# Result tiles worked on in steps, one per product, and later behind their transfer; weight splits three ahead

## The chip, the cores and the metric

The kernel runs on one core of a Trainium2 chip. The metric is the device time of one execution in microseconds.

## The reference

One layer of a hybrid encoder runs over two sequences, a prompt of 512 tokens and a sample of 1024, both 2048 wide, in float32 with shared weights. Cut to what is computed:

```python
h = rms_norm(x, norm_g)
z = h @ w_in                                   # 2048 x 5632
c_val, c_glu, c_gate, q, k, v, a_gate = split(z)   # 1024 x3, 1024, 256, 256, 1024
q, k = rope(q), rope(k)
u = c_val * sigmoid(c_glu)
u = depthwise_conv31(u) + b_dw                 # along the tokens
conv_out = (silu(layer_norm(u)) @ w_pw) * silu(c_gate)
attn_out = banded_sink_attention(q, k, v) * silu(a_gate)   # 8 heads, 2 kv heads, window 128
y = rms_norm(x + concat(conv_out, attn_out) @ w_out)
```

## The kernel before

Every float32 product is made of three passes over operands that are split into a high and a low part (`parts`, L352 on ACT for the high, L353 on DVE for the low part), so weights and activations have to be split before TensorE can use them.

**Units.** The input projection of the sample runs in 44 `Unit`s of 84 matmuls. A unit multiplies a 2 by 2 arrangement of blocks (two columns of weights, two halves of the tokens) by a Strassen-like scheme: seven products (`SUMS`, `OPERAND`) of 12 matmuls each, which accumulate in three PSUM banks (`BANK`: a for the products 0, 2, 4 and 6, b for 1, c for 3 and 5). Four prepared weight tiles feed the seven products: `make0` to `make3` form sums of raw weights on DVE (L136) and split them into one of three hl buffers (`NHL = 3`). After each product `tap` takes the bank's contents: after products 0, 2, 3 and 6 as a copy on ACT into a new result tile (L210), after 1, 4 and 5 as an addition on DVE (L212). Product 6 goes on in the bank that product 4 has filled, so it waits for the tap of product 4; product 5 waits in the same way for the copy of product 3's bank. The taps of a product are issued (`late`) after the first three matmuls of the next product.

**Four stages of units.** The units run in four stages: the convolution's 8 units over the first half of the depth, then over the second half, then the 14 other units (gates, keys, values, queries) over the second half and over the first. In the first and third stage a result tile is stored to DRAM (`part`). In the second and the fourth the unit has a `done`: the other half is added to the result tile in SBUF by an accumulating transfer from GpSimd's queue (`add_into`, L343), and the finished tile is then worked on and stored. In the stages 1, 2 and 4 the first two units are interleaved (`side`).

**The work on a result tile** depends on what it is. For the convolution (`gated`): scaled by the RMS factor R on DVE (L741), Sigmoid on ACT (L742), scaled again on DVE (L743) for the GLU column; multiplied with its partner of the value column (L747) and stored (`h_d`). For gates (`silu_of`): scaled (L756), Silu on ACT (L761), stored. For queries and keys (`rotate`): four DVE instructions of `rope` (L808 to L811), stored. For values (`value_of`): scaled (L756), then transposed by a lane.

**When it is issued.** `tap` puts `[LANDING, done]` on the list `later`. In each product, after the taps and the split of weights, `turn_over` counts all entries down by one and issues those at zero, whole: all of a tile's DVE and ACT instructions, at raised priority (`urgently`, `high_priority(URGENT)`). `turn_over` first calls `mark`, which notes the last instruction so far of DVE and of ACT; whatever is issued in `behind` (the work on result tiles, and the lanes with conv taps, attention and other background work) is put behind these on the same engine. Before the first job, `later` is emptied.

**Order.** A scheduler puts the instructions of each engine in order, by priority and by when buffers come free; the engines then run their queues in that order and wait on semaphores. The `Unit`s prepare weights one ahead: `product` asks for tile i at its start, and at every second product for `i + NHL - 1`, which means up to tile i + 1.

**The rest.** The prompt's projection and the three later parts (`Job`, L484, and `last_run`, L1230) run after the units. Conv taps (L780) are background work on DVE, paced by credit per product. Result tiles live in two pools of four buffers, g and u, that `E` hands out in turn.

Of the kernel before, what the change touches and what calls it, by code (L numbers as in the profile page):

```python
# [32 lines left out]
URGENT = 400  # L33
# [2 lines left out]
SOON = 800  # L36
PM = 30
RUSH = 1.45
LANDING = 3
LOAD = 4500  # L40
SPREAD = 3
RATES = (0.4, 0.6, 0.3, 1.0)
# [2 lines left out]
NT, NRAW, NHL = 28, 3, 3  # L45
# [40 lines left out]
class Unit:  # L86
# [82 lines left out]
    def product(self, step, late):  # L169
        e, nc = self.e, self.e.nc  # L170
        p, o = OPERAND[step]
        i = self.at[p]
        e.w_prep(i + 1)
        hl = e.hl[i]
        n = BANK[step]
        if step in FRESH:
            self.bank[n] = e.PS(self.tags[n], [W])
        acc = self.bank[n]
        toks = e.T[SUMS[step]]
        for j in range(HALF):  # L180
            for q, (l, r) in enumerate(((0, 0), (0, 1), (1, 0))):
                nc.tensor.matmul(  # L182
                    acc,
                    hl[:, l, o, j, :],
                    toks[j][:, r],
                    start=step in FRESH and j == 0 and q == 0,
                    stop=step in LAST and j == HALF - 1 and q == 2,
                    skip_group_check=True,
                )
            if j == 0:  # L190
                for fn in late:
                    fn()

                if step % 2 == self.side:
                    e.w_prep(i + NHL - 1)
                e.turn_over()
            e.tick(3 * MM)
        if step in (1, 3, 5, 6):
            e.hl.pop(i)
        for fn in self.after.get(step, ()):  # L200
            fn()
        return [lambda: e.urgently(self.tap, step)]

    def tap(self, step):
        e, nc = self.e, self.e.nc
        n = ((0, 0), (0, 0), (0, 1), (1, 1), (1, 1), (0, 1), (1, 0))[step]
        bank = self.bank[BANK[step]]
        if step in (0, 2, 3, 6):
            self.d[n] = e.E()
            nc.scalar.activation(self.d[n], bank, AF.Copy)  # L210
        else:
            nc.vector.tensor_tensor(self.d[n], bank, self.d[n], ALU.add)  # L212
        if step in (1, 4, 5, 6):
            part, d = self.part[n[0]][n[1]], self.d.pop(n)
            if self.done:

                e.add_into(d, part)
                e.later.append([LANDING, lambda: self.done(n[0], n[1], d)])
            else:
                e.store(part, d)  # L220

# [51 lines left out]
class Encoder:  # L273
# [108 lines left out]
    def turn_over(self, all=False):  # L382

        self.mark()
        for n, entry in enumerate(self.later):
            entry[0] -= 1
        while self.later and (all or self.later[0][0] <= 0):
            with self.behind():
                self.urgently(self.later.popleft()[1])


    def constants(self):
# [162 lines left out]
class Sequence:  # L555
# [177 lines left out]
    def gated(self, i):  # L733

        e, nc = self.e, self.e.nc
        held, made = {}, []

        def done(t, c, z):
            R = self.R[:, t * W : t * W + W]
            if c == 0:  # L740
                nc.vector.tensor_tensor(z, z, R, ALU.mult)  # L741
                nc.scalar.activation(z, z, AF.Sigmoid)  # L742
                nc.vector.tensor_tensor(z, z, R, ALU.mult)  # L743
            held[t, c] = z
            if (t, 1 - c) in held:
                g, v = held.pop((t, 0)), held.pop((t, 1))
                nc.vector.tensor_tensor(v, v, g, ALU.mult)  # L747
                e.store(self.h_d[i][:, t * W : t * W + W], v)
                made.append(t)
                if len(made) == 2:  # L750
                    e.conv.add(self.taps(i))

        return done
# [4 lines left out]
    def silu_of(self, dst):  # L758
        def done(t, z):
            self.scaled(z, t)  # L760
            self.e.nc.scalar.activation(z, z, AF.Silu)  # L761
            self.e.store(dst[:, t * W : t * W + W], z)

        return done
# [52 lines left out]
    def rotate(self, dst):  # L817
        def done(t, z):
            self.e.store(dst[:, t * W : t * W + W], self.rope(z, t, z))

        return done

# [6 lines left out]
    def value_of(self, g):  # L829
        def done(t, z):  # L830
            self.scaled(z, t)
            self.e.attn.add(self.turn_value(g, t, z))

        return done

# [639 lines left out]
```

## Time and profile before

| | us |
|---|---|
| median of 3 runs | 2267.61 (2260.0 to 2270.22) |
| the profiled execution's own time | 2265.19 |
| its span, first to last instruction | 2263.4 |
| PE busy in the span | 2158.1 |
| DVE busy in the span | 1650.3 |
| ACT busy in the span | 968.8 |
| mean granted TensorE clock | 0.982 |

The profile is of one execution. PE is the matrix engine, PEld its loads of weights, DVE the vector engine, ACT the scalar engine, POOL GpSimd, SP the queue that issues most transfers. A row of the groups gives line, engine, operation, written and read tiles with their shape and the count; then the busy time, the mean in ns of one, and the engine's idle time just ahead of these instructions with what ended it. A row of the waits reads "engine line waited for: us in total, times, longest". A row of the timeline gives the start, the length, engine, line and operation, and in brackets the idle time before it and its releaser. The stages of units end, in this execution, at 180.9, 370.7, 648.1 and 975.0 us.

### The profile page before, as it was taken

The numbers are of one execution on the slowest core, as the hardware profiler recorded it, in microseconds if no ns is written. First come the engines' busy times: TensorE is split into PE (matmuls) and PEld (weight loads), VectorE is DVE, ScalarE is ACT, GpSimd is POOL, SyncE is SP. The second block draws the span as 40 slices with busy tenths as digits, with TensorE's granted clock in tenths as the row PEclk, the third lists the DMA queues.
The fourth block names the chain that finished last, engine by engine and source line by source line (L and its number), as shares of the span: only waits on it lengthen the run. The fifth ranks groups of instructions, "written<-read, shape, count | busy, mean of one in ns | idle before, by whom it ended". The sixth has DMA issues, their size and how long they took to land.

```text
span 2263.4 us, 26350 instructions
## 1 busy us (share of the span) xinstructions
PE 2158.1 (95%) x9510; PEld 1764.4 (78%) x9510; DVE 1650.3 (73%) x2497; ACT 968.8 (43%) x1488; POOL 76.9 (3%) x92
## 2 busy tenths in 40 slices
PE   6999888999999898989999999999999999999998
PEld 5887677788877676778888888888888778888886
DVE  8657777898898788789998668868774586546343
ACT  5465334333353232453444555754463454423232
POOL 0001111000001111100000000000000000000000
PEclk8999999999999999999999999999999999999999
DMA  8967757664566555675444644347543366527342
GB/s 286 321 222 225 192 147 202 243 234 150 185 218 158 144 143 124 166 245 174 163 140 142 203 140 140 131 137 249 196 131 126 130 195 233 172 98 259 104 131 75
DMA packets 207748, 400.12 MB, mean 177 GB/s; under 512 B 18944, under 2 KB 76672, under 8 KB 207616
## 3 DMA queue, kind: packets, MB, share of 16 engines
q1 hardware_dynamic: 194944, 375.35, 49.8%
q0 software_dynamic: 12672, 23.07, 6.5%
q8 instruction: 74, 1.21, 0.2%
q14 instruction: 58, 0.48, 0.1%
HBM read 294.02 MB, written 104.33 MB: 176 GB/s over the span
## 4 chain that ended last, share of the span: by engine, by line
PE 58%; issue 14%; DVE 5%; DMA 4%; POOL 2%; ACT 1%; SPq 0%; POOLq 0%; ACTq 0%; DVEq 0%
PE a L484 20%; PE b L484 10%; PE c L484 10%; PE a L182 3%; PE pv L923 2%; PE a L1230 2%; PE s L1230 2%; DVE f L780 2%; PE s L891 2%; PE c L182 2%; DMA raw<-w_in 1%; PE pt L928 1%; DVE hl L353 1%; PE pv L1230 1%; PE b L1230 1%
## 5 line engine op out<-in xcount | busy, mean ns | idle before, releaser
L353 DVE TENSOR_TENSOR hl<-raw,hl 128x1024 fp32r<-128x1024 f32 (+1 forms) x323 | 371.6, 1150 | 219.6 <-ACT hl L352 210.8
L352 ACT ACTIVATE hl<-raw 128x1024 fp32r<-128x1024 f32 (+1 forms) x323 | 322.7, 999 | 487.3 <-PE a L484 95.0
L182 PE MATMUL a<-t,hl 128*128 128x512 f32 x1968 | 488.2, 401 | 44.3 <-DVE g L212 27.5
L484 PE MATMUL a<-t,hl 128*128 128x512 f32 x2112 | 510.4, 393 | 1.5 <-DVE hl L353 1.5
L182 PEld LDWEIGHTS a<-t,hl 128*128 128x128 f32 x1968 | 379.2, 194 | 134.8 <-DVE g L212 34.5
L780 DVE SCALAR_TENSOR_TENSOR f<-f,c_w_dw,f 128x1024 f32<-128x1024 f32 (+1 forms) x464 | 453.9, 1012 | 2.7 <-ACT f L776 1.6
L484 PEld LDWEIGHTS a<-t,hl 128*128 128x128 f32 x2112 | 393.0, 188 | 80.6 <-DVE hl L353 1.9
L182 PE MATMUL c<-t,hl 128*128 128x512 f32 x984 | 252.2, 405 | 29.7 <-ACT g L210 21.5
L484 PE MATMUL b<-t,hl 128*128 128x512 f32 x1056 | 253.6, 392 | 1.9 <-DVE a L1083 1.9
L484 PE MATMUL c<-t,hl 128*128 128x512 f32 x1056 | 251.9, 391 | 0.0
L182 PEld LDWEIGHTS c<-t,hl 128*128 128x128 f32 x984 | 192.1, 196 | 75.6 <-ACT g L210 24.0
L484 PEld LDWEIGHTS b<-t,hl 128*128 128x128 f32 x1056 | 196.7, 188 | 41.6 <-DVE a L1083 2.3
L484 PEld LDWEIGHTS c<-t,hl 128*128 128x128 f32 x1056 | 197.2, 188 | 40.1 <-DVE a L1083 0.3
L182 PE MATMUL b<-t,hl 128*128 128x512 f32 x492 | 119.4, 391 | 0.0
L182 PEld LDWEIGHTS b<-t,hl 128*128 128x128 f32 x492 | 92.8, 189 | 19.3
L136 DVE TENSOR_TENSOR raw<-raw,raw 128x512 f32<-128x512 f32 x123 | 84.5, 687 | 24.1 <-DMA raw<-w_in 16.2
L210 ACT ACTIVATE u<-a 128x512 f32<-128x512 f32 x76 | 45.2, 595 | 96.0 <-PE a L182 94.0
L905 ACT ACTIVATE p<-p,tiny 128x384 f32<-128x384 f32 (+1 forms) x96 | 54.6, 570 | 52.7 <-DVE tiny L902 52.6
L1230 PE MATMUL a<-hl,t 128*128 128x512 f32 x192 | 74.7, 390 | 0.0
L352 ACT ACTIVATE a<-pt 128x512 fp32r<-128x512 f32 x64 | 38.1, 596 | 79.6 <-PE pt L928 79.5
L353 DVE TENSOR_TENSOR a<-pt,a 128x512 fp32r<-128x512 f32 x64 | 44.0, 687 | 27.4 <-ACT a L352 26.8
L210 ACT ACTIVATE g<-a 128x512 f32<-128x512 f32 x47 | 27.9, 595 | 78.4 <-PE a L182 76.8
(244 smaller groups left out, 2189.5 us busy)
## 6 DMA issues: line engine op xcount, KB each, us to landing
raw<-w_in SPq DMA_DIRECT2D x169, 512.0 KB, 4.5
raw<-w_out SPq DMA_DIRECT2D x64, 512.0 KB, 3.8
raw<-w_out SPq DMA_DIRECT2D x64, 256.0 KB, 3.2
raw<-w_pw SPq DMA_DIRECT2D x24, 512.0 KB, 3.6
f<-xT_s SPq DMA_DIRECT2D x38, 256.0 KB, 5.8
f<-x_s SPq DMA_DIRECT2D x16, 512.0 KB, 6.2
f<-x_p SPq DMA_DIRECT2D x13, 512.0 KB, 6.4
u<-q_d SPq DMA_DIRECT2D x24, 256.0 KB, 4.3
```

Source lines behind the costliest of these rows:

```text
L136: self.e.nc.vector.tensor_tensor(out, x, y, ALU.subtract)
L182: nc.tensor.matmul(acc, hl[:, l, o, j, :], toks[j][:, r], start=step in FRESH and j == 0 and q == 0, stop=step in LAST and j == HALF - 1 a ...
L210: nc.scalar.activation(self.d[n], bank, AF.Copy)
L352: nc.scalar.activation(hi, x, AF.Copy)
L353: nc.vector.tensor_tensor(lo, x, hi.bitcast(F32), ALU.subtract)
L484: nc.tensor.matmul(job.acc[0], hl[:, l, kk // HALF, kk % HALF, :], r, start=i == 0 and p == 0, stop=i == nk - 1 and p == 2,)
L780: nc.vector.scalar_tensor_tensor(t, h[:, j : j + T], w(j), t, ALU.mult, ALU.add)
L891: nc.tensor.matmul(ps[:, 0:n], qs[:, x, h], k[y][:, keys], start=p == 0, stop=p == 2)
L905: nc.scalar.activation(p[:, 0:n], p[:, 0:n], AF.Exp, bias=nm[:, h : h + 1], accum_out=l[:, h : h + 1])
L923: nc.tensor.matmul(pv, v[x][:, vs], pt[:, y], start=i == 0 and p == 0, stop=i == last and p == 2)
L928: nc.tensor.transpose(tp[:, h], p[:, i * P : (i + 1) * P], e.ident)
L1230: nc.tensor.matmul(acc, self.mix[self.KS[i]][:, m, b * P : (b + 1) * P], part[l].rearrange("p a b -> p (a b)"), start=i == 0 and p == 0, s ...
```

## The change

Three things change.

- `done` becomes a generator. Each `turn_over` runs one step of every tile that is due, up to the next `yield`; the yields stand where the work goes from DVE to ACT or back, and at the end of the functions that have no such place. A tile is taken from the list when its generator ends. Tiles that are due no longer wait for the first in the list.
- `LANDING` goes from 3 to 4: the first step of a tile is issued one product later behind the transfer.
- `product` asks for `i + NHL`, up to weight tile i + 2, in every product and not in every second one for up to i + 1.

```diff
-LANDING = 3
+LANDING = 4
...
             if j == 0:
                 for fn in late:
                     fn()
-
-                if step % 2 == self.side:
-                    e.w_prep(i + NHL - 1)
+                e.w_prep(i + NHL)
                 e.turn_over()
...
                 e.add_into(d, part)
-                e.later.append([LANDING, lambda: self.done(n[0], n[1], d)])
+                e.later.append([LANDING, self.done(n[0], n[1], d)])
...
     def turn_over(self, all=False):
 
         self.mark()
-        for n, entry in enumerate(self.later):
+        for entry in list(self.later):
             entry[0] -= 1
-        while self.later and (all or self.later[0][0] <= 0):
-            with self.behind():
-                self.urgently(self.later.popleft()[1])
+            if all or entry[0] <= 0:
+                with self.behind():
+                    with self.tc.high_priority(URGENT):
+                        if next(entry[1], self) is self:
+                            self.later.remove(entry)
...
             if c == 0:
                 nc.vector.tensor_tensor(z, z, R, ALU.mult)
+                yield
                 nc.scalar.activation(z, z, AF.Sigmoid)
+                yield
                 nc.vector.tensor_tensor(z, z, R, ALU.mult)
...
     def silu_of(self, dst):
         def done(t, z):
             self.scaled(z, t)
+            yield
             self.e.nc.scalar.activation(z, z, AF.Silu)
             self.e.store(dst[:, t * W : t * W + W], z)
...
     def rotate(self, dst):
         def done(t, z):
             self.e.store(dst[:, t * W : t * W + W], self.rope(z, t, z))
+            yield
...
         def done(t, z):
             self.scaled(z, t)
             self.e.attn.add(self.turn_value(g, t, z))
+            yield
```

## The prediction

> **What bounds the kernel now.** I read the page first, then a table of the busy time by stage, then in the two stages that stand out the groups by line, the waits, and the timeline of one unit.
>
> ```profile
> span 2263.4 us, 26350 instructions
> PE 2158.1 (95%) x9510; PEld 1764.4 (78%) x9510; DVE 1650.3 (73%) x2497; ACT 968.8 (43%) x1488; POOL 76.9 (3%) x92
> ...
> 56.50:113.10 56.60, 56.60 (x252) 46.88 (x250) 37.54 (x50) 25.14 (x37) 0.00 (x0) 1.00 0.94 321
> ...
> 0.00:180.90 180.90, 163.06 (x677) 130.75 (x678) 125.81 (x197) 99.06 (x154) 0.20 (x4) 0.95 0.79 271
> 180.90:370.70 189.80, 164.89 (x674) 131.87 (x673) 138.67 (x177) 67.78 (x97) 26.70 (x31) 0.94 0.67 178
> 370.70:648.10 277.40, 271.31 (x1180) 221.72 (x1179) 237.97 (x291) 107.81 (x151) 1.28 (x2) 0.99 0.64 212
> 648.10:975.00 326.90, 288.47 (x1194) 232.16 (x1193) 264.85 (x344) 125.26 (x180) 47.86 (x55) 0.95 0.63 160
> 975.00:2263.40 1288.40, 1270.38 (x5793) 1047.86 (x5791) 882.97 (x1491) 568.85 (x907) 0.88 (x1) 1.00 0.49 160
> ```
>
> The windows give length, then busy time and count of PE, PEld, DVE, ACT and POOL, then the granted clock. The kernel is PE's: 95% busy. An undisturbed stretch runs 252 matmuls in 56.6 us, 0.2246 us each. At that price the second stage (674 matmuls) needs 151.4 us and takes 189.8; the fourth (1194) needs 268.2 and takes 326.9. These two, the ones with POOL work, are the only stages where units call `done`, and they lose 38.4 + 58.7 = 97.1 us. The first stage loses some 29 us, mostly its start; the third 277.4 - 265.0 = 12.4; the last, over half the span, loses nothing that this change reaches. DVE has the next claim: 264.85 us of work in the fourth stage against PE's 268.2.
>
> ```profile
> L741 DVE TENSOR_TENSOR g<-g,f 128x512 f32<-128x512 f32 x8 | 5.5, 692 | 10.3 <-DMA g<-part_conv 10.3
> L741 DVE TENSOR_TENSOR u<-u,f 128x512 f32<-128x512 f32 x7 | 4.8, 689 | 5.6 <-DMA u<-part_conv 5.6
> L747 DVE TENSOR_TENSOR u<-u,g 128x512 f32<-128x512 f32 x5 | 3.5, 692 | 14.2 <-DMA u<-part_conv 14.2
> L747 DVE TENSOR_TENSOR g<-g,g 128x512 f32<-128x512 f32 x2 | 1.4, 692 | 2.6 <-DMA g<-part_conv 2.6
> ...
> L756 DVE TENSOR_TENSOR u<-u,f 128x512 f32<-128x512 f32 x17 | 11.7, 690 | 16.9 <-DMA u<-part_q 10.8 <-DMA u<-part_kv 4.6 <-DMA u<-part_gate 1.5
> L756 DVE TENSOR_TENSOR g<-g,f 128x512 f32<-128x512 f32 x16 | 11.0, 691 | 16.3 <-DMA g<-part_q 9.2 <-DMA g<-part_gate 4.7 <-DMA g<-part_kv 2.4
> L808 DVE TENSOR_TENSOR g<-g,f 64x512 f32<-64x512 f32 x10 | 6.9, 687 | 6.9 <-DMA g<-part_q 5.1 <-DMA g<-part_kv 1.5
> L808 DVE TENSOR_TENSOR u<-u,f 64x512 f32<-64x512 f32 x9 | 6.2, 687 | 9.6 <-DMA u<-part_q 7.8 <-DMA u<-part_kv 1.7
> ```
>
> The last field is DVE's idle time ahead of the group: the first readers of a result tile stand waiting for the accumulating transfer, 32.7 us in the second stage (first four rows) and 49.7 in the fourth. DVE idles 189.8 - 138.67 = 51.1 us there in the second and 326.9 - 264.85 = 62.05 in the fourth, so these waits are most of it. Two timelines show how PE pays, first in the second stage, then in the fourth:
>
> ```profile
> 290.93 0.69 DVE L741 TENSOR_TENSOR g<-g,f 128x512 f32<-128x512 f32 x1 [2.05 <-DMA g<-part_conv]
> 291.66 0.63 ACT L742 ACTIVATE g<-g 128x512 f32<-128x512 f32 x1 [6.09 <-DVE g L741]
> 292.19 0.58 ACT L210 ACTIVATE g<-c 128x512 f32<-128x512 f32 x1
> 292.82 4.40 PE L182 MATMUL c<-t,hl 128*128 128x512 f32 x12 [3.18 <-ACT g L210]
> ...
> 822.44 0.88 POOL L343 DMA_DIRECT2D u<-part_q  x1 [9.47 <-DVE u L212]
> 826.25 0.69 DVE L808 TENSOR_TENSOR u<-u,f 64x512 f32<-64x512 f32 x1 [1.09 <-DMA u<-part_q]
> 829.61 1.22 DVE L353 TENSOR_TENSOR hl<-raw,hl 128x1024 fp32r<-128x1024 f32 x1
> 830.74 0.68 DVE L212 TENSOR_TENSOR g<-a,g 128x512 f32<-128x512 f32 x1
> 831.48 7.34 PE L182 MATMUL a<-t,hl 128*128 128x512 f32 x24 [4.09 <-DVE g L212]
> ```
>
> Above, ACT stands six microseconds at the Sigmoid (L742), which waits for DVE, which waits for the transfer; the copy of bank c (L210) is queued behind it, and PE waits for that bank. Below, the transfer issued at 822.44 holds DVE until 826.25, the rotation follows, and the add that frees bank a (L212) ends so late that PE stands 4.09 us. It is a loop: late tap, late transfer, late rotation, next late tap.
>
> ```profile
> PE c L182 <- ACT g L210: 17.8, 5, 6.3
> PE a L182 <- DVE g L212: 23.9, 10, 4.3
> PE s L182 <- ACT hl L352: 7.7, 3, 3.4
> 292.80:296.30 3.50, 3.48 (x9) 0.57 0.00 0
> DMA to landing us min/median/max: 3.8/4.6/8.8
> ```
>
> The first two rows are those stalls, in the second and in the fourth stage; the third, of the whole span, is all that a split's high part cost PE in the paired units. The fourth is the bill behind the first timeline (length, PE busy and count, granted clock): after 3.18 us without work PE got a clock of 0.57 and ran 9 matmuls where 3.5 us hold 15.6, so a stall costs some 1.5 us more than its length. The Trainium skill, "TensorE: Matmul & The Clock Gate", Part 1, says that an idle window of about 3.4 us halves the clock; here 3.18 us already did.
>
> **The change part by part.** I set the instruction order of both built kernels side by side. Counts per engine are equal but for one ACT table load fewer, the conv taps (L780) per stage differ by at most three, and the last 4,886 matmuls of 9,492 with all that stands beside them keep their order. So nothing is added and nothing removed: all of it is order.
>
> *LANDING 4, and steps.* Counting matmuls between the issue of an accumulating transfer and its first reader in the order: L741 median 14 before, 39 after; L808 14.5 and 37; L756 15 and 37; L747 33.5 and 64.5. At 0.2246 us, 14 matmuls are 3.1 us and 37 are 8.3. A landing takes 3.8 to 8.8, so before nearly every reader comes too early and afterwards hardly one does. From DVE's step to ACT's Sigmoid or Silu there are now 10 or 8 matmuls (before 3 and 4.5), from the Sigmoid to L743 18 (before 5): ACT and DVE no longer meet each other's queue in the same product.
>
> DVE then keeps its work and its other waits: second stage 138.67 + (51.1 - 32.7) = 157.1 us, fourth 264.85 + (62.05 - 49.7) = 277.2. Both are above PE's 151.4 and 268.2, so DVE sets the stage. To that I add 4 us in the second and 8 in the fourth, about an eighth of the removed waits (the landings beyond 8 us, and coupling of two engines that are both nearly full): 161 and 285. That saves 29 and 42 us. In the third stage the tail of the second's result tiles lies in the first units; DVE's few microseconds of waits there should go: 2 us.
>
> *Splits three ahead* (`w_prep(i + NHL)` at every step). Costed at nothing: the splits ran at high priority as soon as one of three hl buffers came free, and that limit hasn't moved. From a split's DVE instruction to the first matmul that reads it lie 30 matmuls (median over 176) before and 30 after. In the order the split and the tap's copy (L210) wait for the same product's end, in the paired units too, so neither holds the other up. Were that cover gone, ACT would stand at a split with copies behind it: at one 3.18 us stall with its 1.5 in each of 44 units 206 us. The other bound is a gain, the 7.7 us of splits that PE waited for. I take 0, nearest to the unmoved 30.
>
> *Longer lives of result tiles.* In the query units three of the four now fall in the g buffers (four), where before two did. The copy of step 3's bank takes the buffer of a gate tile whose store is issued 19 matmuls, 4.3 us, earlier:
>
> ```profile
> ag_d<-g SPq DMA_DIRECT2D x16, 256.0 KB, 3.5
> ```
>
> With 3.5 us to landing that fits by 0.8, and bank c is needed one product, 12 matmuls, later still. I take 0; the upper bound is a rival below. POOL's queue keeps its order. On SP the stores of finished tiles (h_d, q_d, ag_d and others) move one to four products later past loads of weights; their readers are the conv lane and the attention. What is still underway when the first job starts is flushed there, and DVE stands for one landing:
>
> ```profile
> DVE g L756 <- DMA g<-part_gate: 4.1, 1, 4.1
> ```
>
> That wait is there already. With up to two products more underway the bounds are 0 and one landing of 8.8; I take 0, as the jobs' matmuls run meanwhile.
>
> Sum: 29 + 42 + 2 = 73 us off the profiled span of 2263.4, so 2190; the execution's own time was 2265.2, 1.8 more than its span, and the median of the runs 2267.6. I forecast **2192 us**.
>
> **The rivals.**
> *DVE keeps the stages.* Over 14 units the fourth stage's DVE work is 264.85 / 14 = 18.9 us a unit and PE's 19.2: it fits by 0.3.
>
> ```profile
> L780 DVE SCALAR_TENSOR_TENSOR f<-f,c_w_dw,f 128x1024 f32<-128x1024 f32 x42 | 53.7, 1279 | 0.0
> ...
> 1075.10:1131.70 56.60, 55.89 (x260) 45.85 (x259) 54.95 (x76) 23.76 (x42) 0.00 (x0) 1.00 0.48 163
> ```
>
> The 42 conv taps are three a unit; a unit that gets a fourth, 1.28 us, doesn't fit. If that lag carries over and the waits move to PE (behind L212) rather than vanish, half of the gain stays: 2265 - 36 = 2229. For it: DVE at 99% of PE's need. Against: the second row, early in the jobs, has DVE 97% busy and PE running all but without a gap.
>
> *Nothing changes.* If the transfer is not what makes DVE late, readers merely wait elsewhere, and the time stays at 2265. The Trainium skill, "DMA: Bandwidth & Descriptors", Anatomy of one DMA, speaks for it: its fit of 2.0 us plus bytes over 436 GB/s would make one of these 256 KB adds land in an estimated 2.6 us, ahead of every reader already. The trace disagrees: no landing under 3.8.
>
> *Slower: the store of a result tile.* If that store lands later than 4.3 us plus the 2.1 that a product leaves beside a copy, ACT stands at L210 with the splits behind it, and PE waits for bank c as in the second stage now: 17.8 us over 5 stalls, 3.6 each, 5.1 with the clock. In 18 units of conv, query, key and value that is 92 us against 73 gained: 2192 + 92 = 2284. It decides from landings of about 6.4 us, against a median of 3.5.
>
> **How the numbers follow.** Forecast (between full recovery to PE's need and two thirds of the sum) 0.72, DVE keeps the stages 0.16, nothing 0.05, slower 0.07. Full recovery is 97 us and a few of the third stage, 2165; that is the low end. The high end takes in the DVE rival: 2232; 0.12 is left beyond it and some below. A measurement of this kernel tells about 0.5%, 11 us, from no change: faster 0.88, same 0.05, slower 0.07.
>
> **What would show it.** Right: the second stage about 161 us, the fourth about 285, their granted clock near 1.00; L741, L747, L756 and L808 with a few microseconds of idle from transfers in place of 82; L742 no longer waiting for L741 for tens of microseconds; later stages within 3 us of 1288. Wrong: PE still waiting for L212 with DVE full (DVE rival), L210 idle before stores (slower), or the same transfer waits at longer distances.

## The result, and the profile after

| | before | after |
|---|---|---|
| median, measured together (4 runs each) | 2263.81 us | 2202.63 us (2200.56 to 2206.52) |
| ratio to before, 95% interval | | 0.973 [0.9698, 0.9761] |
| the profiled execution's own time | 2265.19 us | 2206.52 us |

The change makes the kernel 2.7% faster; the forecast was 2192. In the changed kernel's lines L341 is `add_into`, L350 and L351 are `parts`, L208 and L210 the taps on ACT and DVE, L741, L743, L745 and L749 the convolution's tile work (L741, L742, L743 and L747 before), L758 and L811 the gates' and the rotation's first instructions (L756 and L808).

The page's totals and the table by stage, with the same columns as before:

```profile
span 2204.7 us, 26386 instructions
PE 2137.9 (97%) x9510; PEld 1752.2 (79%) x9510; DVE 1644.3 (75%) x2497; ACT 969.3 (44%) x1487; POOL 77.1 (3%) x92
...
0.00:178.80 178.80, 161.83 (x677) 129.94 (x678) 126.04 (x196) 100.00 (x155) 0.20 (x4) 0.96 0.80 273
178.80:339.00 160.20, 154.13 (x674) 125.70 (x673) 130.32 (x173) 66.89 (x94) 26.29 (x30) 1.00 0.77 211
339.00:614.80 275.80, 270.14 (x1179) 220.32 (x1178) 240.07 (x292) 110.03 (x154) 1.78 (x2) 1.00 0.63 213
614.80:908.00 293.20, 276.09 (x1194) 224.28 (x1193) 263.04 (x345) 122.00 (x176) 48.00 (x55) 0.98 0.66 177
908.00:2204.70 1296.70, 1275.70 (x5792) 1051.98 (x5791) 884.84 (x1496) 570.35 (x909) 0.87 (x1) 0.99 0.49 160
```

The second stage went from 189.8 to 160.2 us, the fourth from 326.9 to 293.2, the first and the third by some 2 each: 67.0 us are gained when the units end. The last stage gives 8.3 back (1288.4 to 1296.7). PE's granted clock rose from 0.94 to 1.00 in the second stage and from 0.95 to 0.98 in the fourth, and for the same 674 and 1194 matmuls PE's busy time fell by 10.8 and 12.4 us. So over a third of the 63.3 us that the two stages gained shows in PE's busy time, and not in standing that is gone.

The groups on DVE that answer to those shown of before, first of the second stage, then of the fourth:

```profile
L741 DVE TENSOR_TENSOR g<-g,f 128x512 f32<-128x512 f32 x8 | 5.5, 683 | 0.0
L741 DVE TENSOR_TENSOR u<-u,f 128x512 f32<-128x512 f32 x7 | 4.8, 686 | 1.0 <-DMA u<-part_conv 1.0
L749 DVE TENSOR_TENSOR u<-u,g 128x512 f32<-128x512 f32 x5 | 3.4, 685 | 1.0 <-DMA u<-part_conv 1.0
L749 DVE TENSOR_TENSOR g<-g,g 128x512 f32<-128x512 f32 x2 | 1.4, 681 | 0.0
L136 DVE TENSOR_TENSOR raw<-raw,raw 128x512 f32<-128x512 f32 x21 | 14.4, 688 | 11.2 <-DMA raw<-w_in 10.2 <-DVE u L741 0.9
```

```profile
L758 DVE TENSOR_TENSOR g<-g,f 128x512 f32<-128x512 f32 x26 | 17.7, 682 | 0.0
L758 DVE TENSOR_TENSOR u<-u,f 128x512 f32<-128x512 f32 x7 | 4.8, 682 | 3.0 <-DMA u<-part_gate 3.0
L811 DVE TENSOR_TENSOR u<-g,f 64x512 f32<-64x512 f32 x11 | 7.6, 687 | 0.7 <-DMA g<-part_kv 0.3 <-DMA g<-part_q 0.2
L811 DVE TENSOR_TENSOR u<-u,f 64x512 f32<-64x512 f32 x9 | 6.2, 688 | 0.3
L136 DVE TENSOR_TENSOR raw<-raw,raw 128x512 f32<-128x512 f32 x36 | 24.8, 689 | 10.9 <-DMA raw<-w_in 9.6 <-DVE g L758 0.7
```

The first readers stood 32.7 and 49.7 us for the accumulating transfer before; now 2.0 and 4.0. But a row that hardly waited before does now: ahead of L136, the sums of raw weights, DVE stands 11.2 and 10.9 us, nearly all of it for a load of raw weights (before: 1.2 and 1.0). A unit's timeline in the second stage, where ACT stood six microseconds at the Sigmoid before:

```profile
275.38 0.69 DVE L741 TENSOR_TENSOR g<-g,f 128x512 f32<-128x512 f32 x1
275.50 5.60 PE L182 MATMUL a<-t,hl 128*128 128x512 f32 x24
...
276.72 0.62 ACT L743 ACTIVATE g<-g 128x512 f32<-128x512 f32 x1
...
280.94 2.88 PE L182 MATMUL b<-t,hl 128*128 128x512 f32 x12
...
281.25 0.68 DVE L745 TENSOR_TENSOR g<-g,f 128x512 f32<-128x512 f32 x1
```

No bracket, so no wait, on any of the three steps, and PE runs on from one product to the next. What PE still waits for, first in the second stage, then in the fourth, and after that the landings of the accumulating transfers:

```profile
PE a L182 <- DVE g L210: 2.7, 3, 1.5
PE a L182 <- ACT g L208: 1.9, 1, 1.9
```

```profile
PE a L182 <- DVE g L210: 8.3, 6, 2.8
PE s L182 <- ACT hl L350: 4.9, 1, 4.9
```

```profile
DMA to landing us min/median/max: 3.7/5.1/9.2
```

PE's 17.8 us for the copies of bank c in the second stage are gone, and of the 23.9 for the tap of bank a in the fourth 8.3 are left. The transfers did not get faster (median 4.6 before, 5.1 now).

### The profile page after: what moved, and what is told of

The parts are those of the page before. It is cut to its first block, busy times and chain, and to the rows that moved or that the text cites. A ratio compares the mean times of both kernels' runs of the same rounds, so it can differ in the third digit from the quotient of the medians.

```text
span 2204.7 us, 26386 instructions
## 1 busy us (share of the span) xinstructions
PE 2137.9 (97%) x9510; PEld 1752.2 (79%) x9510; DVE 1644.3 (75%) x2497; ACT 969.3 (44%) x1487; POOL 77.1 (3%) x92
## 4 chain that ended last, share of the span: by engine, by line
PE 64%; DVE 8%; DMA 6%; issue 3%; ACT 1%; POOL 0%; SPq 0%; DVEq 0%; ACTq 0%; POOLq 0%
PE a L484 19%; PE b L484 10%; PE c L484 10%; PE a L182 7%; PE c L182 2%; DVE f L783 2%; DMA raw<-w_in 2%; PE s L896 2%; PE a L1235 2%; PE s L1235 2%; PE pv L928 2%; DVE hl L351 2%; PE b L182 2%; PE pt L933 1%; DMA u<-q_d 1%
## 5 line engine op out<-in xcount | busy, mean ns | idle before, releaser
L350 ACT ACTIVATE hl<-raw 128x1024 fp32r<-128x1024 f32 (+1 forms) x323 | 323.1, 1000 | 518.1 <-PE a L484 98.6
L351 DVE TENSOR_TENSOR hl<-raw,hl 128x1024 fp32r<-128x1024 f32 (+1 forms) x323 | 371.2, 1149 | 219.4 <-ACT hl L350 210.6
L484 PE MATMUL a<-t,hl 128*128 128x512 f32 x2112 | 510.9, 392 | 0.0
L182 PE MATMUL a<-t,hl 128*128 128x512 f32 x1968 | 475.9, 394 | 27.0 <-DVE g L210 14.4
L182 PEld LDWEIGHTS a<-t,hl 128*128 128x128 f32 x1968 | 370.5, 189 | 113.0 <-DVE g L210 22.5
L484 PEld LDWEIGHTS a<-t,hl 128*128 128x128 f32 x2112 | 392.7, 188 | 78.8
L484 PE MATMUL c<-t,hl 128*128 128x512 f32 x1056 | 252.5, 393 | 0.1
L182 PE MATMUL c<-t,hl 128*128 128x512 f32 x984 | 240.8, 392 | 10.1 <-ACT t L350 5.8
L484 PEld LDWEIGHTS c<-t,hl 128*128 128x128 f32 x1056 | 198.4, 189 | 40.5 <-DVE a L1088 0.4
L182 PEld LDWEIGHTS c<-t,hl 128*128 128x128 f32 x984 | 185.0, 188 | 52.0 <-ACT t L350 7.0
L136 DVE TENSOR_TENSOR raw<-raw,raw 128x512 f32<-128x512 f32 x123 | 84.5, 687 | 47.4 <-DMA raw<-w_in 39.6
L208 ACT ACTIVATE u<-a 128x512 f32<-128x512 f32 x66 | 39.4, 597 | 93.2 <-PE a L182 89.2
L350 ACT ACTIVATE a<-pt 128x512 fp32r<-128x512 f32 x64 | 38.1, 596 | 75.1 <-PE pt L933 75.0
L896 PE MATMUL s<-t,a 128*128 128x384 f32 (+1 forms) x288 | 58.3, 335 | 8.3 <-ACT a L350 6.7
L208 ACT ACTIVATE g<-a 128x512 f32<-128x512 f32 x57 | 34.0, 596 | 70.4 <-PE a L182 67.1
```

The lines of the kernel that those rows point to most:

```text
L136: self.e.nc.vector.tensor_tensor(out, x, y, ALU.subtract)
L182: nc.tensor.matmul(acc, hl[:, l, o, j, :], toks[j][:, r], start=step in FRESH and j == 0 and q == 0, stop=step in LAST and j == HALF - 1 a ...
L350: nc.scalar.activation(hi, x, AF.Copy)
L351: nc.vector.tensor_tensor(lo, x, hi.bitcast(F32), ALU.subtract)
L484: nc.tensor.matmul(job.acc[0], hl[:, l, kk // HALF, kk % HALF, :], r, start=i == 0 and p == 0, stop=i == nk - 1 and p == 2,)
L896: nc.tensor.matmul(ps[:, 0:n], qs[:, x, h], k[y][:, keys], start=p == 0, stop=p == 2)
```

## The experiments

All ratios are to the kernel before, run beside each on the same chip. "Distance" is the median count of matmuls, in the order of the built kernel, between the issue of an accumulating transfer and its first reader, for the four readers L741, L747, L756 and L808 of before; "DVE idle" is what DVE stood for those transfers over the whole span of the profiled execution.

| kernel | distance | DVE idle, us | stage 2 | stage 4 | ratio |
|---|---|---|---|---|---|
| before | 14, 34, 15, 15 | 93.6 | 189.8 | 326.9 | 1 |
| steps alone | 14, 43, 16, 13 | 89.3 | 182.5 | 325.2 | 0.999 [0.9976, 1.0003] |
| splits, LANDING 2 | 17, 33, 18, 15 | 81.8 | 178.8 | 337.6 | 0.9961 [0.9946, 0.9976] |
| LANDING alone | 22, 47, 25, 30 | 46.0 | 169.8 | 298.8 | 0.9811 [0.9791, 0.9832] |
| splits alone | 30, 47, 28, 31 | 35.5 | 163.8 | 304.2 | 0.9804 [0.9784, 0.9823] |
| steps and LANDING | 31, 59, 25, 31 | 54.7 | 167.2 | 303.3 | 0.9803 [0.9785, 0.9821] |
| splits and LANDING | 38, 55, 37, 37 | 10.3 | 168.2 | 293.9 | 0.9744 [0.9721, 0.9767] |
| after (all three) | 39, 65, 37, 37 | 8.0 | 160.2 | 293.2 | 0.973 [0.9698, 0.9761] |
| before, no transfer | | 0 | 156.3 | 278.3 | 0.9601 [0.9578, 0.9623] |

**The splits three ahead, alone.** In the kernel before:

```diff
-                if step % 2 == self.side:
-                    e.w_prep(i + NHL - 1)
+                e.w_prep(i + NHL)
```

> The kernel before with one line of the change: weight tiles asked for up to i + 2 in every product; LANDING 3 and the whole work at once as before. In its instruction order the first readers of a result tile nevertheless stand 28 to 31 matmuls (medians) behind the accumulating transfer where they stood 14 to 15. Theory A (only the distance between transfer and reader counts, however it arises): most of the gain, 2215 to 2228 us. Theory B (as the prediction costed it: splits bring nothing): 2260 to 2268 us. Theory C (DVE and ACT meeting in one product is what costs, so the steps decide): 2255 to 2268 us.

2219.45 us beside 2266.36: 46.9 us from an edit that I had costed at nothing, as theory A said. The splits themselves are not earlier (30 matmuls from a split to its first reader, before and after). What moved is the work on result tiles: `turn_over` puts it behind the newest DVE and ACT instructions, and with the earlier request the newest split is a later one.

**LANDING 4, alone.** `LANDING = 3` becomes 4 in the kernel before.

> The kernel before with LANDING 4 alone. Median distances 22 (L741), 30 (L808), 25 (L756) matmuls. Theory A: waits of DVE for the transfers fall from 82 us to some 25, time 2220 to 2235 us. Theory B: LANDING and steps share the gain, 2220 to 2235 us. Theory C: little, 2248 to 2265 us.

2220.08 us, 46.3 gained, about as much as by the splits. DVE's waits for the transfers in the two stages fell from 82 us to 37, not to the 25 that I expected. Neither reaches the full change's 61.2 by itself, and the two together (57.9, below) are far from their sum of 93: both lengthen the same distance, and a reader that already comes late enough gains nothing from the second.

**The steps, alone.** The `yield`s and the stepping `turn_over` in the kernel before, LANDING 3 and splits as before.

> The kernel before with the steps alone (generators, LANDING 3, splits as before). Distances stay at 13 to 16 matmuls. Theory A: the waits for transfers stay, 2250 to 2266 us. Theory C: most of the gain, 2205 to 2225 us, since ACT no longer stands at a Sigmoid or Silu with a copy queued behind it.

2262.99 us, no difference that can be measured, so theory C is out. In the second stage of the profiled execution the steps give 7 us (182.5); the fourth stays.

**Steps and LANDING, without the splits.** In the kernel after:

```diff
-                e.w_prep(i + NHL)
+                if step % 2 == self.side:
+                    e.w_prep(i + NHL - 1)
```

> The changed kernel with the splits as before: steps and LANDING 4. Median distances 31 (L741), 31 (L808), 25 (L756) matmuls, where the whole change has 37 to 39. Theory A: short of the whole change by the transfers that land after 25 to 31 matmuls (5.6 to 7 us), 2205 to 2218 us. Theory B: the same as the whole change, 2199 to 2206 us.

2218.51 us: without the splits about a quarter of the gain is missing, as theory A said (half a microsecond beyond its range).

**Splits and LANDING, without steps.**

> The changed kernel without the steps: splits three ahead and LANDING 4, a tile's whole work at once as before. Median distances 38 (L741), 37 (L808), 37 (L756) matmuls, as with the whole change; from L741 to the Sigmoid 3 matmuls, as before the change. Theory A (the distance is all): 2200 to 2208 us, the same as the whole change. Theory C (the steps count once the transfers are out of the way): 2212 to 2225 us.

2209.02 us, between the ranges of both theories; its interval overlaps that of the full change. So the steps' share of the total can't be told from nothing, but their place shows. The second stage is 168.2 without and 160.2 with them, as it was 189.8 and 182.5. The waits in the second stage, first of this kernel, then of the changed one (L740 and L739 here are L743 and L741 there), show what differs:

```profile
ACT g L740 <- DVE g L739: 31.5, 6, 6.7
...
ACT u L740 <- DVE u L739: 11.3, 5, 3.6
...
PE a L182 <- DVE g L210: 9.1, 6, 4.0
```

```profile
ACT g L743 <- DVE g L741: 3.6, 4, 1.6
ACT u L743 <- DVE u L741: 1.7, 2, 1.2
```

Issued whole, a tile's Sigmoid still stands in ACT's queue right behind DVE's step, 42.8 us in sum; in steps 5.3 are left. PE pays little of that directly: without steps it does not wait for ACT's copies in this stage at all, but 9.1 us for DVE's tap of bank a (L210), where 2.7 are left with steps. Before the longest of these waits (4.0 us) DVE works off 6 us of tile work, sums of raw weights, a split and two conv taps ahead of that tap. So the steps' gain shows at DVE's tap; that the Sigmoid's wait causes it isn't shown.

**The accumulating transfer left out.** The kernel before without the transfers, everything else in the same order; half of the sums (the other half of the depth) is left out of the result.

```diff
-                e.add_into(d, part)
                 e.later.append([LANDING, lambda: self.done(n[0], n[1], d)])
```

> The kernel before without the accumulating transfer (the half that it would add is left out of the result), everything else in the same order. Theory A: the 82 us that DVE waits for transfers in the second and fourth stage go, with PE's stalls behind them, 2190 to 2212 us. Rival D (tile work that stands early in DVE's order delays the taps with or without a transfer): 2225 to 2255 us.

2176.65 us, 90.3 less than before: a larger gain than theory A's range had, and about the 93.6 us of DVE's idle time for these transfers. Rival D is out.

```profile
181.30:337.60 156.30, 154.44 (x673) 127.06 (x672) 137.37 (x177) 69.25 (x97) 0.00 (x0) 0.99 0.51 167
...
611.40:889.70 278.30, 272.69 (x1194) 223.71 (x1193) 263.26 (x345) 124.88 (x180) 0.00 (x0) 0.99 0.41 138
...
L136 DVE TENSOR_TENSOR raw<-raw,raw 128x512 f32<-128x512 f32 x36 | 24.7, 687 | 0.4
```

Second and fourth stage stand at 156.3 and 278.3 (POOL 0.00), and the last row, L136 in the fourth, does not wait. It is a check of the forecast's sum: DVE's work plus its other waits made 157.1 and 277.2 there. It also shows how far a longer distance alone can go in this order, and the changed kernel is 15 us short of it in the fourth stage.

**Fewer taps of the convolution in the fourth stage.** In the kernel after, `RATES[2]` 0.3 becomes 0.2: 14 fewer DVE instructions there, the taps move to the last stage.

> The changed kernel with the conv lane's rate in the fourth stage at 0.2 in place of 0.3: 30 conv taps there in place of 44, some 18 us of DVE work moved into the jobs. Theory E (a nearly full DVE is what holds the fourth stage at 293 us against PE's 268): the stage takes 280 to 287 us and the kernel 2190 to 2199 us, if the jobs take the taps up. Rival F (single stalls at other waits hold it, not DVE's load): 2199 to 2207 us, stage 290 to 295 us.

2190.01 us, 0.9665 [0.9642, 0.9687]; the fourth stage 285.0, DVE 248.37 in it, as theory E said. The last stage takes the taps at no cost (1287.4). DVE stands as long as before at L136 for raw loads (9.7 us against 9.6 in the changed kernel), but PE's wait for DVE's tap of bank a falls from 8.3 to 2.5 us.

**The rotation's temporary always in a u buffer.** In the kernel after:

```diff
-        b = e.E()
+        b = e.U()
```

> The changed kernel with the rotation's temporary tile always from the u buffers, so that the result tiles of query units alternate between g and u again. Theory G (three result tiles in four g buffers make ACT wait for stores, 7.5 us in the fourth stage, and that costs PE): those waits go, 2194 to 2200 us. Rival: ACT has room for them, 2200 to 2206 us.

2212.33 us, 0.9759 [0.9741, 0.9778], outside both ranges, the fourth stage 302.1. ACT's wait for a gate tile's store, 7.5 us in the changed kernel, is gone from the fourth stage, and yet the stage is 9 us longer. The wait of L136 for raw loads rose there from 9.6 to 15.9 us and PE's wait for DVE's tap from 8.3 to 13.1; why this edit does that isn't shown.

**The stores off SyncE's queue.** In the kernel after, three times:

```diff
-            self.e.store(dst[:, t * W : t * W + W], z)
+            self.e.nc.gpsimd.dma_start(dst[:, t * W : t * W + W], z)
```

> The changed kernel with one edit: the stores of result tiles (the hidden tiles h_d, the gates, the rotated q and k) are issued from GpSimd's queue and no longer from SyncE's, where the loads of raw weight columns stand behind them. Theory S (the wait of VectorE's L136 for a raw load, 16 us over the span before the change and 40 us after it, is a load that stands behind a store whose tile is not ready): that wait falls back below 20 us, the fourth stage from 293 to 283-288 us, the whole to 2190-2198. Rival Q (the wait moves: the accumulating transfers, which are issued on GpSimd too, now stand behind the same stores, and VectorE's and ScalarE's first readers wait for them, over 30 us in sum where 8 to 16 us were): the fourth stage at 293 or over, 2203-2225. Rival N (the raw loads are hidden either way): within 3 us of 2203.

2218.63 us, 0.9777 [0.9751, 0.9803], fourth stage 303.8. My theory S fell: L136's wait rose instead. Three rows of its waits, of SyncE's queue over the whole span, then of DVE and of ACT in the fourth stage:

```profile
SPq L116 <- DVE hl L351: 161.4, 28, 20.1
```

```profile
DVE raw L136 <- DMA raw<-w_in: 18.6, 7, 4.2
```

```profile
ACT g L208 <- DMA ag_d<-g: 28.3, 8, 4.8
```

With no store ahead of it the raw load stands at its own buffer, which DVE's split (L351) has still to read: here the buffer, not a store, sets when it can start. The time is in rival Q's range, but not for its reason: DVE waits for the accumulating transfers hardly longer than in the changed kernel (9.0 us against 8.0). But ACT, which copies into a tile whose store isn't finished, stands 28.3 us where the changed kernel has 7.5.

**The gates' stores from ScalarE, the others from GpSimd.**

```diff
-            self.e.store(dst[:, t * W : t * W + W], z)
+            self.e.nc.scalar.dma_start(dst[:, t * W : t * W + W], z)
```

> As the run with the stores on GpSimd, but the gates' stores are issued from ScalarE, which writes those tiles itself, so that no queue waits for them; the hidden tiles' and the rotated tiles' stores are on GpSimd. Theory S: VectorE's wait for raw loads below 20 us, the whole 2188-2198, and in the fourth stage no more wait for the accumulating transfer than in the changed kernel. Rival Q would now cost less than with all stores on GpSimd: between that run and 2198. Rival N: within 3 us of 2203. If ScalarE's issue of 32 stores itself costs time (its copies free the products' banks), TensorE's wait for ScalarE's L208 grows in the fourth stage and the time is above that of the other run.

2220.29 us, 0.9782 [0.9766, 0.9799], fourth stage 305.3: not better than with all on GpSimd. ACT's wait for the gates' stores is 17.6 us, and L136's 20.7, the most of all. Theory S fell again. Four kernels with the same taps in that stage now line up: L136 waits 9.6, 15.9, 18.6 and 20.7 us and the stage takes 293.2, 302.1, 303.8 and 305.3. That is a correlation: with 14 taps fewer L136 waits 9.7 us too, and the stage takes 285.0.

**Still fewer taps in the third and fourth stage.** In the kernel after:

```diff
-RATES = (0.4, 0.6, 0.3, 1.0)
+RATES = (0.4, 0.5, 0.1, 1.0)
```

> The changed kernel with RATES (0.4, 0.5, 0.1) for (0.4, 0.6, 0.3): of the conv's taps, 18 in place of the changed kernel's 44 run in the fourth stage, and the rest after it, in the jobs of the last stage. Theory E (VectorE is the fullest engine of the fourth stage, 263 us of 293, and what it has too much delays the splits and copies that TensorE waits for; a rate of 0.2 already brought 293 to 285): the fourth stage falls to 278-284 us with VectorE's busy time near 230, the last stage stays at 1287-1297, the whole 2180-2192. Rival L (the last stage has no room for more taps ahead of the jobs that read them): the fourth stage falls likewise, but the last one grows by 8 us or more, the whole 2192-2205. Rival T (what is left of the stage's loss is the transfers' and the raw loads' own, and 0.2 took all that VectorE's load cost): 285 us again, the whole 2188-2192.

```profile
339.10:611.00 271.90, 268.13 (x1179) 220.83 (x1178) 225.31 (x281) 109.25 (x154) 1.78 (x2) 1.00 0.64 213
611.00:890.50 279.50, 272.97 (x1194) 222.77 (x1194) 232.59 (x313) 119.68 (x175) 47.97 (x55) 0.99 0.71 188
890.50:2178.90 1288.40, 1270.98 (x5792) 1048.91 (x5790) 931.89 (x1539) 575.53 (x913) 0.88 (x1) 1.00 0.50 161
```

2184.05 us, 0.9623 [0.9605, 0.964]: the fastest of all versions with the full result, and in each of theory E's ranges. The fourth stage takes 279.5 us, within 1.2 us of that without transfers, the third 271.9, and the last stage has 47 us more DVE work than after the change and is no longer.

**Splits three ahead at the old distance.** The splits alone, but with LANDING 2 in place of 3, so that the distance falls back while the splits are still asked for three ahead.

> The kernel before with the splits asked for three ahead at every product, as in the run of that edit alone, but with LANDING 2 in place of 3: the result tiles' first readers then stand about as far behind their accumulating transfers as before the change (medians 17, 33, 18 and 15 products of 128x128x512 in the issue order for L741, L747, L756 and L808, where the kernel before has 14, 34, 15 and 15 and the splits alone 30, 47, 28 and 31). Theory A (only that distance counts, and the splits three ahead earned 46 us by making it longer): the gain is gone, 2250-2267 us, the second stage 184-190 and the fourth 318-327, and VectorE sits idle for the adds 75-93 us over the span. Rival P (the splits made ahead are themselves what TensorE no longer waits for): 2219-2235, second stage below 172, fourth below 310. Something between, near 2242, would give half to each.

2262.53 us beside 2271.74, 9 of the splits' 46.9 us: the time that theory A gave. The two stages miss its ranges on both sides: the second, 178.8, is shorter, and the fourth at 337.6 is even longer than before. The groups of the fourth stage, with L754 for L756 and L806 for L808:

```profile
L754 DVE TENSOR_TENSOR u<-u,f 128x512 f32<-128x512 f32 x27 | 18.6, 689 | 25.4 <-DMA u<-part_q 15.7 <-DMA u<-part_kv 7.9 <-DMA u<-part_gate 1.8
L806 DVE TENSOR_TENSOR g<-g,f 64x512 f32<-64x512 f32 x11 | 7.6, 687 | 9.2 <-DMA g<-part_q 7.8 <-DMA g<-part_kv 1.4
...
L806 DVE TENSOR_TENSOR g<-u,f 64x512 f32<-64x512 f32 x9 | 6.2, 687 | 14.0 <-DMA u<-part_q 11.9 <-DMA u<-part_kv 2.1
L754 DVE TENSOR_TENSOR g<-g,f 128x512 f32<-128x512 f32 x6 | 4.1, 689 | 8.3 <-DMA g<-part_gate 8.3
```

56.9 us of waits for the transfer are back. The second stage keeps 11 us and the fourth loses as many. Splits three ahead without the distance earn next to nothing; it was the distance.

## Why the prediction was right, and where it was not

**The bound and the mechanism: right.** The first readers came too early behind a transfer whose landing takes 4 to 9 us, and DVE, ACT and PE paid in turn. Ordered by DVE's idle time the table's ratios fall nearly in line, whichever edit made the distance, and without the transfer the two stages take 156.3 and 278.3, within 1.1 us of DVE's work and other waits in my sum (157.1 and 277.2). My reading of the order (14 before, 37 to 39 after) was that of the whole change, so the sum was good although its shares were not.

**The second stage: 161 forecast, 160.2.** Partly by luck. The waits for the transfer fell by 30.7 where I had 28.7, and DVE has 8.4 us less work in the stage (130.32 for 138.67; 2.1 of it turned up in the third); against that stand the 10 us that L136 now waits.

**The fourth stage: 285 forecast, 293.2.** This is the term that was mis-sized. I had DVE's work, 264.85, its other waits unchanged at 12.35, and 8 for waits that stay, so 20.35 us of idle. Measured: 293.2 - 263.04 = 30.2. The waits for the transfer that stay are 4.0; L136 waits 9.9 us more than before, and nothing in my sum had a place for that. I had checked the splits' readers (30 matmuls, unmoved) and not what the sums of raw weights wait for. These waits come with the splits three ahead once the transfers are out of the way: in the fourth stage 9.6 and 10.1 us with splits and LANDING (with steps and without), 3.1 with the splits alone, 0.9 with the splits and LANDING 2, at most 1.1 in the kernels without them. The changed kernel's timeline shows how PE pays (DVE's rows between the first and the second, 6 us of work without a gap, are left out):

```profile
834.39 0.69 DVE L136 TENSOR_TENSOR raw<-raw,raw 128x512 f32<-128x512 f32 x1 [3.55 <-DMA raw<-w_in]
...
841.26 0.68 DVE L210 TENSOR_TENSOR g<-a,g 128x512 f32<-128x512 f32 x1
...
842.00 1.63 PE L182 MATMUL a<-t,hl 128*128 128x512 f32 x4 [2.75 <-DVE g L210]
```

Four of the five waits of L136 in this stage are followed so, within 8 us, by a wait of PE for the tap of bank a: 5.9 of its 8.3 us. With 14 taps fewer in the stage L136 waits as long (9.7), but PE only 2.5 at that tap. This fits a late raw load costing PE time only where DVE has no room to catch up.

**Splits three ahead at nothing: wrong.** The reason held (the splits can't be earlier than their buffer), the conclusion didn't: the request moves the point behind which the tiles' work is issued. Alone it is worth 46.9 us, on top of steps and LANDING some 16 (0.9803 to 0.973).

**The steps.** They took the Sigmoid's wait, as I said, and some 8 us of the second stage, though PE's part of that shows at DVE's tap. Alone they leave ACT 36.2 of 61.8 us at the Sigmoid, since DVE's step ahead of it still waits for the transfer. In the total this doesn't show.

**Longer lives of result tiles at 0, and the slower rival.** ACT does wait for the gates' stores (7.5 us over three in the changed kernel), but the edit that removed this wait did not shorten the stage. Where the stores were issued from another queue, the wait grew to 28.3 us, with the fourth stage 10.6 us longer, though L136's waits grew in the same runs; the two can't be separated. The slower rival's mechanism exists, but not at anything like the 92 us that I gave it: even there PE waited 3.4 us for copies of bank c in that stage.

**DVE keeps the stages.** I gave it 2229 us and 0.16. It did not take half of the gain, but a part: taking 30 us of taps off the fourth stage's DVE shortened the stage by 13.7 us, PE's waits for DVE's tap from 8.3 to 2.7 and L136's waits from 9.6 to 5.8. My counter-argument, that PE runs on with DVE at 97% early in the jobs, didn't carry over to the units; no run shows why.

**Nothing changes.** No transfer landed under 3.7 us in any of these kernels, so the estimate of 2.6 us that I worked out from the Trainium skill, "DMA: Bandwidth & Descriptors", Anatomy of one DMA, is not what this transfer takes.

**Later stages within 3 us: missed by 5.** The last stage took 1287 to 1298 us over all these kernels with hardly a change in its order, and the steps alone had 1297.7. The changed kernel's profiled execution is the longest of its four. So the 8.3 us given back are within what single profiles of this stage scatter; I don't claim a cause.

**What stays open** is what would bring the raw loads earlier. A load can start when DVE has split what lay in its buffer: in the changed kernel one such split ends at 746.10 us, the load is issued at 746.12, and L136 stands for it until 751.69. But a fuller DVE doesn't by itself make these waits longer: with 14 taps fewer they stayed at 9.7 us, with 26 fewer they fell to 5.8. No run had a fourth raw buffer.

## What to carry to other kernels

When a consumer stands waiting for a transfer, count in the built order how many matmuls lie between issue and first use, and compare their time with the landing times of the trace: that one distance ordered the gains here, whichever edit produced it. An edit that moves "the newest instruction so far" moves everything that is anchored to it, so cost such an edit by its effect on the order and not by what it prepares. Once the wait is gone, look at which engine is full and take movable work off it: two numbers in a table of rates took the ratio from 0.973 to 0.9623.

## What the runs showed of the hardware

In the changed kernel the same accumulating transfer of 256 KB took from 3.7 to 9.2 us to land (up to 9.6 over all runs), so a distance that fits the median still leaves waits: with LANDING alone (medians of 22 to 47 matmuls, 4.9 us and more) 46 us of DVE's idle time were left, with 37 and more (8.3 us) eight to ten.

Leaving all 88 of these transfers out gave 90.3 us back, which is about what DVE had stood waiting for them (93.6). So little is left for their own issue and traffic; most of their price was that they came late. The match isn't exact bookkeeping: from the changed kernel, with 8.0 us of such waits left, to the one without transfers the ratio still falls by 0.013, some 29 us, and there L136's waits are short as well (2.4 and 0 us in the two stages) and the DMA engines have less to move (busy share 0.41 in the fourth stage, 0.63 before).

A wait of PE of some 2 us can already lower its clock. Between 60 and 975 us the kernel before has 18 waits of PE of 1.5 to 4.4 us. After the four of up to 1.76 us the next 3.4 us ran at a granted clock of 1.00; after 13 of the 14 from 1.97 us up they ran at 0.50 to 0.66. There is no sharp limit: after 2.02 us in the changed kernel the clock stayed at 1.00.
